# FFN up: the third pair of columns as plain products instead of seven block products

## The chip, the cores and the metric

The kernel runs on one core of one Trainium2 chip. The metric is the device time of one execution in microseconds (us). TensorE (PE in the profile) multiplies, VectorE (DVE) and ScalarE (ACT) do the elementwise work, GpSimd (POOL) very little, and SyncE (SP) issues the loads. Each engine runs its instructions in the order of its own queue, and semaphores join them.

## The reference, cut to what matters

The reference is a trunk of two layers on 512 tokens of 1024 features, all in float32. Each layer has a mixer (attention and a state space model in layer 0, a gated recurrence in layer 1) and a feed-forward block (FFN), with an RMS norm before and after each:

```python
def swiglu(x, w_gate, w_up, w_down):
    return (jax.nn.silu(x @ w_gate) * (x @ w_up)) @ w_down

        hn = rms_norm(x, norm_ffn_pre[layer])
        ff = swiglu(hn, ffn_w_gate[layer], ffn_w_up[layer], ffn_w_down[layer])
        x = x + rms_norm(ff, norm_ffn_post[layer])
```

`w_gate` and `w_up` are 1024 x 2816 each, so there are 22 blocks of 128 gate columns and 22 blocks of 128 up columns. One gate block and the up block of the same number are called a pair here, numbered from 0 to 21. The change touches the two products `x @ w_gate` and `x @ w_up`, in both layers.

## The kernel before

**Numbers in two parts.** The kernel keeps x transposed: `xT` is 8 tiles of 128 features by 512 tokens. For a product in full precision each operand is split into a rounded part (`hi`, written by ScalarE as fp32r) and the rest (`lo`, a subtraction on VectorE). `mm3` (line 275) then makes three matmuls: hi with hi, hi with lo, lo with hi. For x the parts are `xh` and `xl`, for the weights `whi` and `wlo`. A `Chunk` (line 221) is a split weight block: 1024 x 128 weights lie in two tiles of 128 x 512, so one block costs two copies on ScalarE (L240) and two subtractions on VectorE (L241). A `Raw` (line 205) is such a block as loaded, two loads of 256 KB.

**Plain pairs.** The first four blocks, pairs 0 and 1, are computed plainly: 8 steps over the features, three matmuls each, 512 tokens wide. `half_cols` (line 555) does this in two halves of 256 tokens, because the norm before it delivers x in halves; the first half runs inside `out_proj`, the second in `gemm_cols` (line 571). `gemm_cols` is a generator: it stops after the second half, and what follows (the evacuation of the four banks, and further plain blocks if its list is longer) is done when `ffn_up` runs it on, at line 678.

**Block pairs.** From pair 2 on, the two blocks of a pair are treated as one product of 2 x 2 blocks (two halves of the features, gate and up, two halves of the tokens) by the Strassen-Winograd scheme with 7 block products instead of 8. `pair_weights` (line 636) loads both blocks, makes four sums of weight blocks on VectorE (L644 to L647), and splits the seven weight blocks: `a` (gate), `c` and `b` (sums) and `d` (what is left of up). The products need sums of x too: t1, t2, t3, t4, made once per layer in the loop at line 659. ScalarE writes two scaled tiles `xa`, `xb` per step, VectorE makes four sums (L666 to L669), and the sums are split into `th`, `tl` (L673, L674). The sum `t0` becomes t1: its two parts are written over the second half of `xh[k]` and `xl[k]` for k from 0 to 3, which the plain pairs have then read.

Each of the seven products is 4 steps of three matmuls, 256 wide (line 690). They go into four PSUM banks in the order 11, t2, t1, 21, t3, 22, t4 as the program is written; ScalarE copies three partial results out (L707, L709, L711) and VectorE combines them in seven operations of 128 x 256 (L720 to L726). `gated` (line 613) applies the activation and multiplies gate by up into a `hh` tile (L616).

**Buffers.** The split weights and raw blocks live in a list of named buffers, `places`: 22 in the pool `sb` and 10 in the pool `hp` of the layer, later joined by those `hh` buffers whose hidden tile comes late. `place` takes the first one free in program order (or the first one in `sb` if asked), and a load into a buffer waits until its last reader is done. Pair 2's split weights are the exception: they have `hh` buffers of their own (the iterator `own`, line 650), and its raw blocks come from `sb`, so that they can be loaded early.

**Order.** The program is written in dependence order, and a scheduler of the framework fixes the order of each engine's queue ahead of time by priorities (program order) and modelled times. Around the norm (in `out_proj`) the order is pinned by hand; in the up phase it isn't. On the chip each queue runs in that fixed order, whatever is late.

Of the kernel before, what the change touches and what calls it, by code (L numbers as in the profile page):

```python
# [11 lines left out]
F32 = mybir.dt.float32  # L12
F32R = mybir.dt.float32r
I32 = mybir.dt.int32
AF = mybir.ActivationFunctionType
ALU = mybir.AluOpType
# [3 lines left out]
P = 128  # L20
S = 512
D = 1024
NF = D // P
NT = S // P
HID = 2816
NH = HID // P
# [68 lines left out]
def hybrid_trunk(  # L95
# [9 lines left out]
    dve, act, pool = nc.vector, nc.scalar, nc.gpsimd  # L105
    sb = ctx.enter_context(tc.tile_pool(name="sb", bufs=1))
# [14 lines left out]
    def bank(name, use="main"):  # L121
        q = sets[use]
        q.append(q.pop(0))
        return psum.tile([P, 512], F32, tag=f"bank{q[-1]}", name=name)
# [16 lines left out]
    def step_one():  # L141
        due, _, gen = heapq.heappop(steps)
        clock[0] = max(clock[0], due)
        try:
            start(gen, next(gen))
        except StopIteration:
            pass

    def tick():
        while steps and steps[0][0] <= clock[0]:  # L150
            step_one()
# [34 lines left out]
    HT = S // 2  # L186
# [12 lines left out]
    def give(ps):  # L199
        places.extend(p for p in ps if p not in retired)  # L200
# [55 lines left out]
    def wchunk(src, nk, n, nm, **kw):  # L256
        return Chunk(Raw(nk, n, nm, src), nm, **kw)

    def wcols(w, c0, nk, nm, **kw):

        return wchunk(w[:, c0:c0 + P].rearrange("(k p) n -> p k n", p=P), nk, P, nm, **kw)
# [286 lines left out]
        return dve.scalar_tensor_tensor(l, src, g, h.bitcast(F32), op0=ALU.mult, op1=ALU.subtract)  # L548

    NFIRST = 4  # L550

    def first_cols(lst, nm, eng=None):
        return [wcols(w, c0, NF, f"{nm}{i}", base=sb, eng=eng) for i, (w, c0) in enumerate(lst[:NFIRST])]

    def half_cols(h, ws, xh, xl, bs, nm):

        if bs is None:
            bs = [bank(f"{nm}b{i}") for i in range(NFIRST)]
        for k in range(NF):
            while (h, k) not in ready:  # L560
                step_one()
            for i in range(NFIRST):
                for j, w in enumerate(ws[i](k)):
                    pe.matmul(bs[i][:, HS[h]], lhsT=w, rhs=xh[k][:, HS[h]], start=(k + j == 0), stop=False)
                tick()
            for i in range(NFIRST):
                pe.matmul(bs[i][:, HS[h]], lhsT=ws[i](k)[0], rhs=xl[k][:, HS[h]], start=False, stop=(k == NF - 1))
                tick()
        return bs

    def gemm_cols(lst, first, xh, xl, nm, evac):

        ws, bs = first
        half_cols(1, ws, xh, xl, bs, nm)
        for w2 in ws:
            w2.free()
        yield
        for i in range(NFIRST):
            evac(i, bs[i])
        for i in range(NFIRST, len(lst)):  # L580
            w2 = wcols(lst[i][0], lst[i][1], NF, f"{nm}{i}")
            b = bank(f"{nm}b{i}")
            for k in range(NF):
                mm3(b, w2(k), xh[k], xl[k], k == 0, k == NF - 1)
            w2.free()
            evac(i, b)
# [11 lines left out]
    def ffn_up(layer, xh, xl, first, nsum, nm, hp):  # L598
# [4 lines left out]
        cols2 = ffn_cols(layer)  # L603
        hidden = []
        env = {}
        HK = NF // 2
# [22 lines left out]
                act.activation(env[n][1], b, AF.Copy)  # L629
                gated(*env[n], n)  # L630

        heads = gemm_cols(cols2[:NFIRST], first, xh, xl, nm, evac)
        next(heads)
        mid()

        def pair_weights(n, alloc=None, base=None):

            r0, r1 = [Raw(NF, P, f"{nm}{n}{i}", cols2[2 * n + i][0][:, n * P:(n + 1) * P].rearrange(
                "(k p) n -> p k n", p=P), base=base) for i in range(2)]
            (a11, a12), (a21, a22) = r0.parts, r1.parts  # L640
            rs = Raw(NF, P, f"s_{nm}{n}", base=base)
            rt = Raw(HK, P, f"t_{nm}{n}")
            (s1, s4), (s2,) = rs.parts, rt.parts
            dve.tensor_tensor(s1, a21, a22, op=ALU.add)  # L644
            dve.tensor_tensor(s2, s1, a11, op=ALU.subtract)  # L645
            dve.tensor_tensor(a21, a11, a21, op=ALU.subtract)
            dve.tensor_tensor(s4, a12, s2, op=ALU.subtract)  # L647
            return [Chunk(t, f"{nm}{n}{q}", alloc=alloc) for t, q in ((r0, "a"), (rs, "c"), (r1, "d"), (rt, "b"))]

        own = iter([*range(11, NH), 3, 4, 5, 6])  # L650
        for q in range(NFIRST // 2 + 3):
            retired.add((hp, f"hh{q}"))
        wa, wc, wd, wb = pair_weights(
            NFIRST // 2, lambda name: hp.tile([P, S], F32R, tag=f"hh{next(own)}", name=name), sb)


        t1 = [(xh[k][:, HS[1]], xl[k][:, HS[1]]) for k in range(HK)]
        th, tl = [], []
        for k in range(HK):
            a = hp.tile([P, S], F32, tag=f"hh{7 + k % 2}", name=f"xa_{nm}{k}")  # L660
            b = hp.tile([P, S], F32, tag=f"hh{9 + k % 2}", name=f"xb_{nm}{k}")
            act.activation(a, xT[k], AF.Copy, scale=col("g1", layer * NF + k))
            act.activation(b, xT[k + HK], AF.Copy, scale=col("g1", layer * NF + k + HK))
            raw = Raw(4, HT, f"tr_{nm}{k}")
            (t2, t3), (t4, t0) = [(t[:, 0], t[:, 1]) for t in raw.parts]
            dve.tensor_tensor(t0, a[:, HS[1]], a[:, HS[0]], op=ALU.subtract)  # L666
            dve.tensor_tensor(t3, b[:, HS[1]], a[:, HS[1]], op=ALU.subtract)
            dve.tensor_tensor(t2, b[:, HS[1]], t0, op=ALU.subtract)
            dve.tensor_tensor(t4, t2, b[:, HS[0]], op=ALU.subtract)  # L669
            h = hp.tile([P, 3, HT], F32R, tag="tq", bufs=8, name=f"th_{nm}{k}")  # L670
            l = hp.tile([P, 3, HT], F32R, tag="tq", bufs=8, name=f"tl_{nm}{k}")
            for src, hi, lo in ((raw.parts[0], h[:, 0:2], l[:, 0:2]), (t4, h[:, 2], l[:, 2]), (t0, *t1[k])):
                act.activation(hi, src, AF.Copy)  # L673
                dve.tensor_tensor(lo, src, hi.bitcast(F32), op=ALU.subtract)  # L674
            raw.free()
            th.append(h)
            tl.append(l)
        for _ in heads:
            pass
        give([(hp, f"hh{q}") for q in range(7, NH)])  # L680
        X = {
            "11": [(xh[k][:, HS[0]], xl[k][:, HS[0]]) for k in range(HK)],
# [8 lines left out]
            for k in range(HK):  # L691
                mm3(o[:, HS[0]], w2(k0 + k), x[k][0], x[k][1], k == 0 and not onto, k == HK - 1, skip_group_check=onto)

        for n in range(NFIRST // 2, NH):
            if n > NFIRST // 2:
                for q in range(n + 3):
                    retired.add((hp, f"hh{q}"))
                places[:] = [p for p in places if p not in retired]
                wa, wc, wd, wb = pair_weights(n)
            b0, b1, b2 = [bank(f"{nm}{i}b{n}") for i in range(3)]  # L700
            b3 = side(f"{nm}3b{n}")
            e = sb.tile([P, S], F32, tag="sq", bufs=2, name=f"pu_{nm}{n}")
            p5 = sb.tile([P, HT], F32, tag="sqh", bufs=2, name=f"pv_{nm}{n}")
            p1, p6 = e[:, HS[0]], e[:, HS[1]]

            product(b0, wa, 0, X["11"])
            act.activation(p1, b0[:, HS[0]], AF.Copy)  # L707
            product(b1, wb, 0, X["t2"])
            act.activation(p6, b1[:, HS[0]], AF.Copy)  # L709
            product(b2, wc, 0, X["t1"])  # L710
            act.activation(p5, b2[:, HS[0]], AF.Copy)  # L711
            product(b0, wa, HK, X["21"], onto=True)
            product(b1, wd, 0, X["t3"], onto=True)
            product(b2, wc, HK, X["22"], onto=True)
            product(b3, wd, HK, X["t4"])
            for w2 in (wa, wc, wd, wb):
                w2.free()
            gt, ut = out_tiles(n)
            rb = env["rb"]
            dve.tensor_tensor(p6, p1, p6, op=ALU.add)  # L720
            dve.tensor_tensor(gt[:, HS[0]], b0[:, HS[0]], rb[:, HS[0]], op=ALU.mult)
            dve.tensor_tensor(p1, p1, b1[:, HS[0]], op=ALU.add)
            dve.tensor_tensor(ut[:, HS[1]], p1, p5, op=ALU.add)
            dve.tensor_tensor(p6, p6, b2[:, HS[0]], op=ALU.add)
            dve.tensor_tensor(gt[:, HS[1]], p6, rb[:, HS[1]], op=ALU.mult)
            dve.tensor_tensor(ut[:, HS[0]], p1, b3[:, HS[0]], op=ALU.subtract)  # L726
            gated(gt, ut, n)

        hh, hl = [], []
        for n in range(NH):  # L730
            if n < 4:
                h, _ = place(f"hi_{nm}{n}", F32R, hp)
            elif n < 16:
                h = sb.tile([P, S], F32R, tag="xh" if n < 12 else "xl", bufs=NF, name=f"hi_{nm}{n}")
            else:
                h = hp.tile([P, 3, HT], F32R, tag="tq", bufs=8, name=f"hi_{nm}{n}")
                h = h.rearrange("p a n -> p (a n)")[:, 0:S]
            act.activation(h, hidden[n], AF.Copy)
            if n == 0:
                l = place(f"lo_{nm}{n}", F32R, hp)[0]  # L740
            else:
                l = hp.tile([P, S], F32R, tag=f"hh{n - 1}", name=f"lo_{nm}{n}")
# [885 lines left out]
    xh, xl, first, nsum = even_layer()  # L1628
    for f in range(NF):
        dump(f"x1_{f}", xT[f])  # L1630
    xh, xl, first, nsum = ffn(0, xh, xl, first, nsum)
# [4 lines left out]
    xh, xl, first, nsum = odd_layer(xh, xl, first, nsum)  # L1636
# [34 lines left out]
```

## Time and profile before

| | us |
|---|---|
| median of 3 runs (1167.83 to 1178.44) | 1168.26 |
| the profiled execution | 1169.77 |
| its span, first to last instruction | 1167.7 |
| first block product of layer 0, pair 2 | 292.5 |
| first block product of layer 1, pair 2 | 827.9 |

A group line of the profile names the source line, the engine, the operation, the output and inputs by their tile names, shapes and a count. The banks of the block products are called f00b to f03b in layer 0 and f10b to f13b in layer 1; the plain pairs use mo0b and mo1b. A weight tile such as whi_f03c is the hi part of block c of pair 3 in layer 0. A stretch line gives, for each engine, busy time and number of instructions, then the granted TensorE clock, the share of the DMA engines and GB/s. A wait line reads: who waited, for whom, total, times, longest. TensorE's busy time is modelled: a matmul of 256 columns is shown with about 0.28 us, while the next one starts about 0.12 us after it; the distance of the starts is what counts. In square brackets stands the idle time before an instruction and what ended it.

### The profile page before, as it was taken

The numbers are of one execution on the slowest core, as the hardware profiler recorded it, in microseconds if no ns is written. First come the engines' busy times: TensorE is split into PE (matmuls) and PEld (weight loads), VectorE is DVE, ScalarE is ACT, GpSimd is POOL, SyncE is SP. The second block draws the span as 40 slices with busy tenths as digits, with TensorE's granted clock in tenths as the row PEclk, the third lists the DMA queues.
The fourth block names the chain that finished last, engine by engine and source line by source line (L and its number), as shares of the span: only waits on it lengthen the run. The fifth ranks groups of instructions, "written<-read, shape, count | busy, mean of one in ns | idle before, by whom it ended". The sixth has DMA issues, their size and how long they took to land.

```text
span 1167.7 us, 20255 instructions
## 1 busy us (share of the span) xinstructions
PE 1131.7 (97%) x7550; PEld 1013.2 (87%) x7550; DVE 876.8 (75%) x1841; ACT 626.6 (54%) x1290; POOL 60.6 (5%) x100
## 2 busy tenths in 40 slices
PE   6999899999999999999999999999999999999997
PEld 6877666889999999988889887889999999988886
DVE  7989675478999899882345887956999899984224
ACT  7556576357655555652244479744855455582221
POOL 1000010003000000000004000004000000000001
PEclk9999989999999999999999999999999999999999
DMA  8534410522333332423330323430253333334221
GB/s 211 144 117 134 108 45 1 172 64 63 93 109 100 101 99 83 125 92 96 121 100 1 106 86 98 126 109 1 77 146 95 101 109 91 90 119 126 91 63 72
DMA packets 165561, 113.45 MB, mean 97 GB/s; under 512 B 26852, under 2 KB 142296, under 8 KB 165464
## 3 DMA queue, kind: packets, MB, share of 16 engines
q1 hardware_dynamic: 162168, 109.95, 32.2%
q10 hardware_dynamic: 3040, 2.17, 0.7%
q8 instruction: 59, 0.97, 0.3%
q14 instruction: 38, 0.31, 0.1%
q0 software_dynamic: 256, 0.06, 0.0%
HBM read 103.75 MB, written 4.19 MB: 92 GB/s over the span
## 4 chain that ended last, share of the span: by engine, by line
PE 82%; DVE 5%; ACT 5%; DMA 4%; issue 2%; POOL 0%; ACTq 0%; DVEq 0%; POOLq 0%; SPq 0%
PE fo L170 10%; PE op_fd L170 10%; PE op_mo L170 6%; PE f00b L170 5%; PE f02b L170 5%; PE f01b L170 4%; PE f11b L170 4%; PE f10b L170 4%; PE f12b L170 4%; PE qkv L170 4%; PE gg L170 3%; PE f03b L170 2%; PE f13b L170 2%; PE mo1b L170 2%; PE mo0b L170 2%; PE xbb L170 2%
## 5 line engine op out<-in xcount | busy, mean ns | idle before, releaser
L241 DVE TENSOR_TENSOR wlo_fo<-wraw_fo,whi_fo 128x512 fp32r<-128x512 f32 x44 | 30.3, 691 | 63.8 <-PE fo L170 58.7
L170 PE MATMUL op_fd<-hi_f,whi_fd 128*128 128x512 f32 (+1 forms) x200 | 73.7, 369 | 0.0
L170 PE MATMUL op_fd<-lo_f,whi_fd 128*128 128x512 f32 (+1 forms) x200 | 73.4, 367 | 0.0
L170 PE MATMUL op_fd<-hi_f,wlo_fd 128*128 128x512 f32 (+1 forms) x200 | 73.0, 367 | 0.0
L170 PE MATMUL fo<-wlo_fo,hi_f 128*128 128x512 f32 x176 | 69.4, 394 | 0.0
L170 PE MATMUL fo<-whi_fo,lo_f 128*128 128x512 f32 x176 | 69.1, 394 | 0.0
L170 PE MATMUL fo<-whi_fo,hi_f 128*128 128x512 f32 x176 | 68.9, 396 | 0.0
L240 ACT ACTIVATE whi_fo<-wraw_fo 128x512 fp32r<-128x512 f32 x44 | 27.6, 631 | 70.6 <-DMA wraw_fo<-in_ffn_w_down_dram 43.4
L241 DVE TENSOR_TENSOR wlo_fd<-wraw_fd,whi_fd 128x512 fp32r<-128x512 f32 x44 | 30.1, 690 | 46.4 <-ACT whi_fd L240 42.5
L240 ACT ACTIVATE whi_fd<-wraw_fd 128x512 fp32r<-128x512 f32 x44 | 27.4, 629 | 54.7 <-DMA wraw_fd<-in_ffn_w_down_dram 33.8
L170 PEld LDWEIGHTS op_fd<-lo_f,whi_fd 128*128 128x128 f32 x200 | 37.7, 189 | 6.8
L170 PEld LDWEIGHTS op_fd<-hi_f,wlo_fd 128*128 128x128 f32 x200 | 37.7, 189 | 6.7
L170 PEld LDWEIGHTS op_fd<-hi_f,whi_fd 128*128 128x128 f32 x200 | 37.7, 189 | 6.6
L170 PE MATMUL qkv<-whi_qkv,xh_m 128*128 128x512 f32 x96 | 40.5, 427 | 0.0
L170 PEld LDWEIGHTS fo<-whi_fo,lo_f 128*128 128x128 f32 x176 | 33.1, 188 | 7.8
L170 PEld LDWEIGHTS fo<-whi_fo,hi_f 128*128 128x128 f32 x176 | 33.1, 188 | 7.7
L170 PEld LDWEIGHTS fo<-wlo_fo,hi_f 128*128 128x128 f32 x176 | 33.1, 188 | 7.5
L170 PE MATMUL qkv<-wlo_qkv,xh_m 128*128 128x512 f32 x96 | 38.3, 399 | 0.0
L170 PE MATMUL qkv<-whi_qkv,xl_m 128*128 128x512 f32 x96 | 38.0, 396 | 0.0
L644 DVE TENSOR_TENSOR wraw_s_f<-wraw_f,wraw_f 128x512 f32<-128x512 f32 x40 | 27.4, 684 | 11.4 <-DMA wraw_f<-in_ffn_w_up_dram 10.7
L241 DVE TENSOR_TENSOR wlo_mo<-wraw_mo,whi_mo 128x512 fp32r<-128x512 f32 x32 | 21.4, 686 | 14.5 <-ACT whi_mo L240 14.2
L645 DVE TENSOR_TENSOR wraw_t_f<-wraw_s_f,wraw_f 128x512 f32<-128x512 f32 x40 | 27.3, 682 | 6.0 <-DMA wraw_f<-in_ffn_w_gate_dram 6.0
(1974 smaller groups left out, 4297.8 us busy)
## 6 DMA issues: line engine op xcount, KB each, us to landing
wraw_f<-in_ffn_w_gate_dram SPq DMA_DIRECT2D x88, 256.0 KB, 3.1
wraw_f<-in_ffn_w_up_dram SPq DMA_DIRECT2D x88, 256.0 KB, 3.3
wraw_fd<-in_ffn_w_down_dram SPq DMA_DIRECT2D x44, 256.0 KB, 2.8
wraw_fo<-in_ffn_w_down_dram SPq DMA_DIRECT2D x44, 256.0 KB, 2.9
wraw_qkv<-in_ev_w_in_dram SPq DMA_DIRECT2D x24, 256.0 KB, 3.5
wraw_mo<-in_ev_w_out_dram SPq DMA_DIRECT2D x16, 256.0 KB, 4.3
wraw_xb<-in_od_w_in_dram SPq DMA_DIRECT2D x16, 256.0 KB, 2.8
wraw_gg<-in_od_w_in_dram SPq DMA_DIRECT2D x16, 256.0 KB, 2.8
```

Source lines behind the costliest of these rows:

```text
L170: self.pin(nc.tensor.matmul(o, lhsT=lhsT, rhs=rhs, start=start, stop=stop, **kw))
L240: act.activation(hi, src, AF.Copy)
L241: eng.tensor_tensor(lo, src, hi.bitcast(F32), op=ALU.subtract)
L644: dve.tensor_tensor(s1, a21, a22, op=ALU.add)
L645: dve.tensor_tensor(s2, s1, a11, op=ALU.subtract)
```

## The change

Pair 2 joins the plain pairs. `gemm_cols` gets the first six blocks instead of four; the two new ones come ready made as `plain`, two `Chunk`s that are made where pair 2's block weights were made, with raw blocks from `sb` and split parts in eight `hh` buffers (before, pair 2's seven split blocks took fourteen). Pair 3 is now the first block pair; its weights are prepared after the block sums of x, before the evacuations, from the common list of buffers. Since the plain products of pair 2 read both halves of `xh` and `xl`, t0 can't be split at once any more: it is kept in two buffers of its own (`z`), and its split into t1 stands behind the plain products.

```diff
     NFIRST = 4
+    NPLAIN = 3
...
-    def gemm_cols(lst, first, xh, xl, nm, evac):
+    def gemm_cols(lst, first, xh, xl, nm, evac, ready_w=None):
...
         for i in range(NFIRST, len(lst)):
-            w2 = wcols(lst[i][0], lst[i][1], NF, f"{nm}{i}")
+            w2 = ready_w(i) if ready_w else wcols(lst[i][0], lst[i][1], NF, f"{nm}{i}")
             b = bank(f"{nm}b{i}")
...
-        heads = gemm_cols(cols2[:NFIRST], first, xh, xl, nm, evac)
+        heads = gemm_cols(cols2[:2 * NPLAIN], first, xh, xl, nm, evac, lambda i: plain[i - NFIRST])
...
-        own = iter([*range(11, NH), 3, 4, 5, 6])
-        for q in range(NFIRST // 2 + 3):
+        own = iter(range(11, NH))
+        for q in range(NPLAIN + 3):
             retired.add((hp, f"hh{q}"))
-        wa, wc, wd, wb = pair_weights(
-            NFIRST // 2, lambda name: hp.tile([P, S], F32R, tag=f"hh{next(own)}", name=name), sb)
+        plain = [Chunk(Raw(NF, P, f"{nm}p{i}", cols2[i][0][:, cols2[i][1]:cols2[i][1] + P].rearrange(
+            "(k p) n -> p k n", p=P), base=sb), f"{nm}p{i}",
+            alloc=lambda name: hp.tile([P, S], F32R, tag=f"hh{next(own)}", name=name))
+            for i in range(NFIRST, 2 * NPLAIN)]
...
+        z = Raw(HK, HT, f"tz_{nm}")
+        z0 = [z.parts[k // z.step][:, k % z.step] for k in range(HK)]
         for k in range(HK):
...
-            (t2, t3), (t4, t0) = [(t[:, 0], t[:, 1]) for t in raw.parts]
+            (t2, t3), (t4, _) = [(t[:, 0], t[:, 1]) for t in raw.parts]
+            t0 = z0[k]
...
-            for src, hi, lo in ((raw.parts[0], h[:, 0:2], l[:, 0:2]), (t4, h[:, 2], l[:, 2]), (t0, *t1[k])):
+            for src, hi, lo in ((raw.parts[0], h[:, 0:2], l[:, 0:2]), (t4, h[:, 2], l[:, 2])):
                 act.activation(hi, src, AF.Copy)
                 dve.tensor_tensor(lo, src, hi.bitcast(F32), op=ALU.subtract)
...
+        wa, wc, wd, wb = pair_weights(NPLAIN)
         for _ in heads:
             pass
+
+        for k in range(HK):
+            act.activation(t1[k][0], z0[k], AF.Copy)
+            dve.tensor_tensor(t1[k][1], z0[k], t1[k][0].bitcast(F32), op=ALU.subtract)
+        z.free()
         give([(hp, f"hh{q}") for q in range(7, NH)])
...
-        for n in range(NFIRST // 2, NH):
-            if n > NFIRST // 2:
+        for n in range(NPLAIN, NH):
+            if n > NPLAIN:
```

## The prediction

> **What bounds the kernel now.** I read the page's first part and its chain of waits, then the busy times in stretches of 10 us through both FFN up phases, then what TensorE waited for at the start of each phase, and last the queues of VectorE, ScalarE and SyncE there.
>
> ```profile
> span 1167.7 us, 20255 instructions
> PE 1131.7 (97%) x7550; PEld 1013.2 (87%) x7550; DVE 876.8 (75%) x1841; ACT 626.6 (54%) x1290; POOL 60.6 (5%) x100
> PE 82%; DVE 5%; ACT 5%; DMA 4%; issue 2%; POOL 0%; ACTq 0%; DVEq 0%; POOLq 0%; SPq 0%
> ```
>
> TensorE sets the time, so an edit pays only where it removes TensorE work or a hole in it. This edit adds TensorE work; the holes must pay for it. In the stretches below the first pair of numbers is TensorE's busy time and its count of matmuls. At 340 to 350 us the up phase runs without a hole.
>
> ```profile
> 300.00:310.00 10.00, 9.33 (x76) 8.86 (x74) 10.00 (x18) 6.91 (x13) 0.00 (x0) 1.00 0.24 69
> 310.00:320.00 10.00, 8.65 (x70) 8.46 (x71) 9.56 (x20) 4.65 (x10) 0.00 (x0) 1.00 0.49 143
> 340.00:350.00 10.00, 10.00 (x86) 10.00 (x85) 10.00 (x20) 5.91 (x14) 0.00 (x0) 1.00 0.30 86
> 470.00:480.00 10.00, 9.18 (x77) 8.97 (x76) 9.64 (x19) 4.75 (x11) 0.00 (x0) 1.00 0.36 105
> 830.00:840.00 10.00, 7.96 (x62) 7.31 (x61) 9.75 (x19) 9.97 (x21) 0.00 (x0) 1.00 0.07 19
> 850.00:860.00 10.00, 9.52 (x79) 9.32 (x79) 10.00 (x21) 5.51 (x11) 0.00 (x0) 1.00 0.62 173
> 860.00:870.00 10.00, 9.87 (x83) 9.68 (x82) 10.00 (x21) 6.09 (x13) 0.00 (x0) 1.00 0.30 83
> 980.00:990.00 10.00, 9.20 (x77) 9.00 (x77) 10.00 (x21) 5.77 (x12) 0.00 (x0) 1.00 0.24 69
> ```
>
> Against 86 matmuls per 10 us, the start of layer 0's phase lacks 10 + 16 = 26 and that of layer 1 lacks 24 + 7 + 3 = 34. I count missing matmuls rather than idle time, because after each stop the next matmuls also come further apart than in a full stream. VectorE, the third pair of numbers, is full in nearly all of these stretches. What ended the holes (first two rows layer 0, the others layer 1):
>
> ```profile
> PE f02b L170 <- ACT whi_f03c L240: 1.0, 1, 1.0
> PE f01b L170 <- ACT pu_f L709: 1.0, 1, 1.0
> PE f11b L170 <- DVE tl_f L674: 1.1, 1, 1.1
> PE f13b L170 <- DVE ut_f L726: 0.5, 1, 0.5
> PE f10b L170 <- ACT pu_f L707: 0.5, 1, 0.5
> PE f10b L170 <- DVE wlo_f13a L241: 0.4, 1, 0.4
> ```
>
> These are weight splits, block sums of x and evacuations: work of VectorE and ScalarE that is late at the start of the phase.
>
> **The change part by part.** *TensorE.* Per layer, 7 products of 4 k-steps of 3 matmuls, 84 of 256 columns, give way to 2 columns of 8 k-steps of 3, 48 of 512 columns. Both prices stand in the chain:
>
> ```profile
> 353.06 1.43 PE f01b L170 x12
> 655.13 22.15 PE xbb L170 x96
> ```
>
> A 256-wide one takes 1.43/12 = 0.119 us and a 512-wide one 22.15/96 = 0.231 us. So 48 x 0.231 = 11.07 us stand against 84 x 0.119 = 10.01 us: +1.06 us per layer, +2.1 us for both, all of it on the path. The Trainium skill, page "TensorE: Matmul & The Clock Gate", section "Back-to-back issue gap", gives columns/2.4 + 2.5 ns, thus 215.8 and 109.2 ns; by it the edit would add 1.19 us per layer and the sum below would be 0.3 us worse. The trace's 231 and 119 ns lie above both figures, so the rows stand.
>
> *The holes.* 26 + 34 = 60 missing matmuls x 0.119 = 7.1 us (3.1 and 4.0). Whether they close is a matter of VectorE's ledger. Prices, from the chain, are 0.60 us for a 512-wide operation (1.20 for two) and 0.34 for a 256-wide one:
>
> ```profile
> 835.29 1.20 DVE gt_f L627 x2
> 850.88 0.34 DVE pu_f L720
> 279.77 0.68 DVE L645 TENSOR_TENSOR wraw_t_f<-wraw_s_f,wraw_f 128x512 f32<-128x512 f32 x1
> 284.38 0.41 DVE L666 TENSOR_TENSOR wraw_tr_f<-xa_f 128x256 f32<-128x256 f32 x1
> 304.89 0.42 DVE L674 TENSOR_TENSOR tl_f<-wraw_tr_f,th_f 128x256 fp32r<-128x256 f32 x1
> 292.75 1.45 PE f00b L170 x12
> ```
>
> In layer 0 the block sums start at 284.38 and end at 304.89. From 284.38 until TensorE can begin pair 4, VectorE now owes: block sums 4 x (6 x 0.34 + 0.60) = 10.6; the last two splits of pair 2, 1.2; four sums and seven splits each for pairs 3 and 4, 13.2; evacuation of the first two pairs, 2.4; that of pair 2, 7 x 0.34 + 0.60 = 3.0. In all 30.4 us, done at 314.8. TensorE without holes would reach pair 4 at 292.7 + 2 x 10.0 = 312.7, so VectorE is about 2 us late, which fits the 3.1 us lost. After the change pair 2 costs 4 splits instead of 4 sums and 7 splits before that point, and 1.2 of evacuation. Of those 11 operations 7 lay in VectorE's queue from 279.77 up to the first block sum, 4.2 us, where now 4 lie, 2.4 us; so the block sums can begin 1.8 us sooner, at 282.6. Then it owes: block sums without t0's split 4 x (5 x 0.34 + 0.60) = 9.2; pairs 3 and 4, 13.2; three plain evacuations, 3.6; the four moved splits, 1.4. In all 27.4, done at 310.0, while TensorE reaches pair 4 at 292.7 + 11.1 + 10.0 = 313.8. Two us late become almost 4 us early, and pair 3 too has 11 us of plain matmuls as cover. ScalarE loses 7 + 3 copies per layer and gains 4 + 1; it was not full in layer 0 after 300 us. I take the holes as closed, but keep one stop of 0.4 us per layer, the smallest of the waits above, for the new seam between plain and block products: 7.1 - 0.8 = 6.3 us back. Bounds: nothing back, to all 7.1.
>
> *The moved split.* Four ScalarE copies and four VectorE subtractions of 256 columns per layer now wait for the plain products, since they overwrite the second half of xh and xl.
>
> ```profile
> 832.08 0.41 ACT L673 ACTIVATE xh_mo<-wraw_tr_f 128x256 fp32r<-128x256 f32 x1
> 833.07 0.42 DVE L674 TENSOR_TENSOR xl_mo<-wraw_tr_f,xh_mo 128x256 fp32r<-128x256 f32 x1
> ```
>
> They touch k 0 to 3 only, so the last matmul that they wait for is 4 k-steps, 12 x 0.231 = 2.8 us, before the end of the plain ones. One copy and four subtractions take 0.41 + 4 x 0.42 = 2.1 us, and the products 11 and t2 stand ahead of t1, 2 x 1.43 us more. Queued behind them are the evacuation of the third pair and the splits of pair 4, both with slack by the ledger. I take 0; if this cover went, the price is a late tl_f as in the row of 1.1 us above, per layer.
>
> *Loads and buffers.* The third pair still loads four blocks of 256 KB through SyncE; POOL gets nothing. Two buffers more are held for t0 until the moved splits. Pair 3's gate blocks take the two sb buffers left free, but its up blocks must, as I read the order of the list, wait for buffers of the first columns.
>
> ```profile
> 287.60 4.30 SPq L216 DMA_DIRECT2D wraw_f<-in_ffn_w_up_dram  x3
> wraw_f<-in_ffn_w_up_dram SPq DMA_DIRECT2D x88, 256.0 KB, 3.3
> 826.94 3.19 DMA wraw_f<-in_ffn_w_up_dram
> 830.25 0.69 DVE L644 TENSOR_TENSOR wraw_s_f<-wraw_f,wraw_f 128x512 f32<-128x512 f32 x1 [1.06 <-DMA wraw_f<-in_ffn_w_up_dram]
> 831.19 1.02 DVE L674 TENSOR_TENSOR tl_f<-wraw_tr_f,th_f 128x512 fp32r<-128x512 f32 x2
> ```
>
> In layer 1 such a load held VectorE for 1.06 us at 829, and tl_f, behind it in the queue, is what TensorE then waited for. After the change the load may be as late, but pair 3 is wanted 11 us later: 0, bounded by the same wait.
>
> **Sum.** +2.1 - 6.3 = -4.2 us. The profiled execution took 1169.77 us (its span of 1167.7 and 2.1 around it), so 1165.6 on its scale; the median of the runs shown is 1168.26, 1.5 us lower, and I predict for it: 1168.26 - 4.2 = 1164.1 us.
>
> **The rivals.** *The queue's order holds TensorE, not the amount of work.* Then a late load or copy in a strict queue stops it as before, and the longer matmuls come on top. For it speaks the wait of 1.06 us above, and that ScalarE was far from full at 310 to 320 (4.65 of 10). Against it: VectorE had under half a microsecond free per 10 us there. Nothing comes back: +2.1, 1170.4 us, slower than before. It decides once less than 2.1 of the 7.1 us returns. The same page of the Trainium skill ("Architectural detail") has VectorE and ScalarE as strict first-in first-out; the trace agrees, tl_f at 831.19 running only behind the blocked sum.
>
> *The stop moves to the seam.* Pair 3's up blocks come late and hold VectorE in front of the block sums, or t1 is late: one stop per layer like the one of 1.1 us, with 0.3 for the restart. That is 1.4 instead of 0.4 twice: -2.2, 1166.0 us. For it: SyncE's three issues at 287.60 took 4.30 us, waiting for buffers. Against it: the 11 us of cover.
>
> *The lead lasts.* VectorE's lead also closes the late holes at 470 to 480 and 980 to 990, 9 matmuls each, 18 x 0.119 = 2.1 us, and no seam is left: 2.1 - 7.1 - 2.1 = -7.1, 1161.1 us. Against it: 100 us of full VectorE lie between, in which pairs cost it 11 x 0.60 + 7 x 0.34 + 0.60 = 9.6 of TensorE's 10.0 us, so a lead would grow, but those waits may come from buffers.
>
> **How the numbers follow.** Forecast 0.50, seam 0.22, order of the queues 0.15, lasting lead 0.13. The range runs from the lasting lead, 1161.0, to 1168.5, halfway between the seam and the queue rival, and leaves out 0.15. Faster or slower by over 1%, which is about what a measurement of this kernel can tell from no change, means 11.7 us. No case comes near it: the holes hold 9.2 us together, the added work is 2.1. I leave 0.01 for faster and 0.02 for slower, for an order of instructions that turns out otherwise in a whole phase.
>
> **What would show it.** Right: 48 matmuls of 128x512 in about 11.1 us ahead of f03 and f13; no TensorE wait above 0.5 us in the 30 us behind them; block sums done some 10 us sooner than 304.89; VectorE no longer full in those stretches. Wrong: waits of about 1 us on f0 or f1 banks behind whi, tl or pu; a first t1 product held by xl; TensorE's busy time up by 2 us with the same counts of missing matmuls.

## The result and the profile after

The kernel before took 1171.28 us and the changed one 1165.95 us (medians of 18 runs each); the ratio is 0.9944, 95% interval 0.9922 to 0.9966, that is 6.6 us less with 4 to 9 as its bounds; the medians differ by 5.3 us. The prediction was 1164.1 us, 4.2 less than a start of 1168.26, the median of 3 runs; the 18 runs put that start 3.0 us higher. Two later comparisons beside the kernel before gave 0.993 and 0.9935. One run of e2, an experiment below, took 3862.53 us and one of b4 2822.71; both are left out of all figures.

The first part and the summary of the chain, from the page of the changed kernel:

```profile
span 1165.9 us, 20079 instructions
PE 1135.2 (97%) x7478; PEld 1014.8 (87%) x7478; DVE 865.5 (74%) x1815; ACT 623.5 (53%) x1280; POOL 60.2 (5%) x100
PE 86%; ACT 5%; DMA 4%; DVE 3%; issue 1%; ACTq 0%; POOL 0%; DVEq 0%; POOLq 0%; SPq 0%
```

TensorE's busy time rose by 3.5 us with 72 matmuls fewer, VectorE's fell by 11.3, and VectorE's share of the chain went from 5% to 3%. The plain pair in the chain of waits of the changed kernel, layer 1 as the example (start, length, matmuls):

```profile
829.42 11.20 PE f1b L170 x48
```

The same kernel in stretches (TensorE's busy time and its matmuls come first):

```profile
300.00:310.00 10.00, 10.00 (x71) 9.27 (x70) 10.00 (x20) 9.25 (x19) 0.00 (x0) 1.00 0.12 35
310.00:320.00 10.00, 10.00 (x86) 10.00 (x85) 10.00 (x20) 5.32 (x11) 0.00 (x0) 1.00 0.46 133
470.00:480.00 10.00, 7.74 (x51) 7.33 (x50) 7.14 (x14) 3.77 (x8) 0.00 (x0) 0.83 0.29 83
...
1010.00:1020.00 10.00, 8.62 (x71) 8.22 (x71) 8.78 (x17) 6.03 (x13) 0.00 (x0) 1.00 0.34 108
```

The starts of both up phases are full: 71 matmuls from 300 to 310 because some are still 512 wide, then 86. The late holes are still there, and in this execution that of layer 0 is larger than before (51 matmuls for 77). What TensorE waited for from 440 to 520 us, and the one wait that counts in layer 1:

```profile
PE f00b L170 <- ACT whi_f021a L240: 2.0, 1, 2.0
PE f01b L170 <- ACT pu_f L721: 0.7, 2, 0.5
...
PE f12b L170 <- ACT whi_f120c L240: 1.3, 1, 1.3
```

**Where the time went, by phase.** A phase is read from the broadcast of the norm (bc_f, eight matmuls in each layer) to the last matmul of the down product. The row of bc_f gives the first of the eight in layer 0 and the last of the eight in layer 1, which starts 0.8 us behind that layer's first in each of these kernels. The rows of the kernel before, then of the changed one (smallest, median and largest duration in ns, first and last start in us):

```profile
L170 PE MATMUL bc_f<-cst,rsy_f x16: 272/275/275, 291.7 to 827.9; 128*128 128x128 f32 x16
...
L170 PE MATMUL op_fd<-hi_f,wlo_fd x200: 277/392/422, 494.8 to 622.8; 128*128 128x512 f32 x76, 128*128 128x256 f32 x24
...
L170 PE MATMUL fo<-whi_fo,lo_f x176: 387/394/400, 1034.9 to 1160.5; 128*128 128x512 f32 x176
```

```profile
L170 PE MATMUL bc_f<-cst,rsy_f x16: 272/275/275, 291.5 to 829.1; 128*128 128x128 f32 x16
...
L170 PE MATMUL op_fd<-hi_f,wlo_fd x200: 279/392/401, 493.2 to 624.5; 128*128 128x512 f32 x76, 128*128 128x256 f32 x24
...
L170 PE MATMUL fo<-whi_fo,lo_f x176: 387/393/402, 1031.3 to 1158.7; 128*128 128x512 f32 x176
```

Layer 0 took 622.8 - 291.7 = 331.1 us before and 333.0 after, layer 1 332.6 and 329.6. Read in the same way, with c0 as a second profile of the kernel before and a0 and c1 as two more of the changed one (the experiments below):

| us | before, c0 | after, a0, c1 | change predicted |
|---|---|---|---|
| layer 0, up and down | 331.1, 331.0 | 333.0, 329.1, 332.9 | 1.06 - 3.1 + 0.4 = -1.6 |
| layer 1, up and down | 332.6, 332.7 | 329.6, 329.0, 329.2 | 1.06 - 4.0 + 0.4 = -2.5 |

Layer 1 gained 3.0 to 3.7 us, a little more than predicted. Layer 0 gained 2.0 once and lost 1.9 twice. By these two lines the median should have moved by 1 to 6 us. A part of the rest lies ahead of layer 0's phase.

**A gain that the prediction did not have.** VectorE's timeline of the kernel before, at the end of the mixer of layer 0, 40 us ahead of the up phase (in brackets the idle time ahead of an instruction and what ended it):

```profile
250.33 0.69 DVE L644 TENSOR_TENSOR wraw_s_f<-wraw_f,wraw_f 128x512 f32<-128x512 f32 x1 [2.25 <-DMA wraw_f<-in_ffn_w_up_dram]
250.94 0.42 DVE L532 TENSOR_TENSOR oacc_mo<-oacc_mo,oqs_mo 128x256 f32<-128x256 f32 x1
```

L644 is the first weight sum of the third pair. It stands in VectorE's queue among the mixer's last sums and waits 2.25 us for a load; oacc_mo behind it is late, and TensorE waits for it (waits of the kernel before, 240 to 262 us):

```profile
PE cs_mo L170 <- DVE oacc_mo L532: 0.9, 1, 0.9
PE cs_mo L170 <- ACT oqs_mo L530: 0.5, 1, 0.5
```

TensorE's busy time from 244 to 292 us, first before, then in a0, a run of the changed kernel; both had the full clock there:

```profile
244.00:292.00 48.00, 45.62 (x382) 44.96 (x381) 35.89 (x85) 29.30 (x68) 14.41 (x17) 1.00 0.21 61
```

```profile
244.00:292.00 48.00, 47.01 (x393) 46.42 (x392) 35.90 (x86) 31.27 (x70) 14.41 (x17) 1.00 0.21 62
```

A plain pair has no such sum, so 1.4 us of idle time go. All four profiles here that have the third pair in blocks (before, c0, e1, e2) have the wait on oacc_mo, 0.8 to 2.0 us; none with it plain has it. In layer 1 the same L644 stands at 780.68 and cost TensorE only 0.3 us.

### The profile page after: what moved, and what is told of

The parts are those of the page before. It is cut to its first block, busy times and chain, and to the rows that moved or that the text cites. A ratio compares the mean times of both kernels' runs of the same rounds, so it can differ in the third digit from the quotient of the medians.

```text
span 1165.9 us, 20079 instructions
## 1 busy us (share of the span) xinstructions
PE 1135.2 (97%) x7478; PEld 1014.8 (87%) x7478; DVE 865.5 (74%) x1815; ACT 623.5 (53%) x1280; POOL 60.2 (5%) x100
## 4 chain that ended last, share of the span: by engine, by line
PE 86%; ACT 5%; DMA 4%; DVE 3%; issue 1%; ACTq 0%; POOL 0%; DVEq 0%; POOLq 0%; SPq 0%
PE fo L170 10%; PE op_fd L170 10%; PE op_mo L170 7%; PE f10b L170 5%; PE f00b L170 4%; PE f11b L170 4%; PE f01b L170 4%; PE f12b L170 4%; PE f02b L170 4%; PE qkv L170 4%; PE gg L170 3%; PE f13b L170 2%; PE f03b L170 2%; PE mo0b L170 2%; PE fd0b L170 2%; PE xbb L170 2%
## 5 line engine op out<-in xcount | busy, mean ns | idle before, releaser
L617 DVE TENSOR_TENSOR hh_f<-ut_f,gt_f 128x512 f32<-128x512 f32 x44 | 30.2, 685 | 1.6 <-ACT gt_f L615 1.5
```

Of the source, the lines that this page charges most:

```text
L617: dve.tensor_tensor(h, ut, gt, op=ALU.mult)
```

## The experiments

All ratios are to the kernel before, measured beside the run, and are ratios of mean times. The last column is read from the profiled execution as above.

| run | edit | us, median | ratio, 95% interval | layers 0 + 1, us |
|---|---|---|---|---|
| before | | | 1 | 331.1 + 332.6 |
| a0 | the changed kernel | 1161.99 | 0.993 [0.9905, 0.9955] | 329.1 + 329.0 |
| e1 | before, pair 10 plain instead of the third | 1167.76 | 0.9984 [0.9961, 1.0006] | 331.5 + 332.3 |
| e2 | before, block sums on GpSimd | 1179.94 | 1.0082 [1.005, 1.0114] | 337.6 + 339.3 |
| e3 | changed, 12 more VectorE operations per layer | 1172.73 | 1.0034 [1.0008, 1.006] | 333.7 + 331.4 |
| b1 | changed, one more buffer | 1157.37 | 0.9853 [0.9822, 0.9885] | 329.3 + 326.9 |
| b2 | changed, hidden buffers kept longer | 1158.94 | 0.9877 [0.9853, 0.9901] | 330.2 + 328.2 |
| b3 | changed, fourth pair plain too | 1159.34 | 0.9879 [0.9847, 0.9911] | 328.4 + 328.1 |
| b4 | changed, pair 10 plain too | 1157.01 | 0.9871 [0.9835, 0.9908] | 328.8 + 328.6 |
| c0 | before again | 1168.00 | 0.9978 [0.9948, 1.0008] | 331.0 + 332.7 |
| c1 | changed again | 1163.93 | 0.9935 [0.9907, 0.9964] | 332.9 + 329.2 |
| c2 | b1 again | 1160.20 | 0.9885 [0.9843, 0.9927] | 328.9 + 326.8 |
| c3 | b3 again | 1154.40 | 0.9855 [0.9818, 0.9892] | 328.4 + 328.0 |

### The changed kernel again

> The changed kernel once more, beside the kernel before. Ledger theory (VectorE owes the start of each up phase about 6 us less): ratio 0.994 to 0.997, the first 30 us behind the plain pair free of TensorE waits above 0.5 us in both layers again, and a late hole again before pair 21's first product, because its load waits for a buffer that pair 19 frees. Rival (the late hole was an accident of one execution): the waits behind whi_f021a and whi_f120c fall under 0.5 us in this trace.

The starts were full again, and the ratio agrees. The late hole of layer 0 was not the same; it is taken up below.

### Was it VectorE's work or the order of the queues?

*e1* leaves the third pair in blocks and computes pair 10 plainly (there the second half of x is partly the block sum, so two columns have other values):

```diff
                 places[:] = [p for p in places if p not in retired]
+                if n == 10:
+                    for i in (2 * n, 2 * n + 1):
+                        w2 = wcols(cols2[i][0], cols2[i][1], NF, f"{nm}p{i}")
+                        o = bank(f"{nm}b{i}")
+                        for k in range(NF):
+                            mm3(o, w2(k), xh[k], xl[k], k == 0, k == NF - 1)
+                        w2.free()
+                        evac(i, o)
+                    continue
```

> The kernel before with pair 10 computed plainly instead of pair 2 (its second token half meets t1 in place of x for half of the features, so the outputs differ; the work is the same in size). The same TensorE work is added and the same VectorE work removed, but 80 us behind the start. Ledger theory: the holes at the start stay (26 and 34 missing matmuls), the plain pair costs its 1.2 us per layer, so +2 to +3 us against before, ratio 1.001 to 1.004. Rival (VectorE is relieved anywhere, the place does not matter): as the change, ratio 0.994 to 0.997.

The ratio came out between the two. Stretches of e1:

```profile
300.00:310.00 10.00, 8.10 (x66) 7.62 (x65) 9.81 (x19) 5.04 (x11) 0.00 (x0) 1.00 0.58 164
470.00:480.00 10.00, 10.00 (x87) 10.00 (x86) 10.00 (x21) 7.08 (x14) 0.00 (x0) 1.00 0.35 98
```

The start's hole stayed, as the ledger said, but this doesn't speak for the ledger alone: TensorE's order at the start is that of the kernel before, with waits on the same two tiles (whi_f03c 0.9 us, pu_f 1.0), and any cause that lies there would have stayed. The phase also began 4.6 us sooner, so the two stretches aren't quite the same work. The late hole went, which neither theory had. The added 2.4 us and the late holes about cancel. So place matters: here a plain pair closed a hole behind it, not those ahead.

*e2* takes the block sums off VectorE in another way, with TensorE's work as before:

```diff
-            dve.tensor_tensor(t0, a[:, HS[1]], a[:, HS[0]], op=ALU.subtract)
+            pool.tensor_tensor(t0, a[:, HS[1]], a[:, HS[0]], op=ALU.subtract)
...
-            dve.tensor_tensor(t4, t2, b[:, HS[0]], op=ALU.subtract)
+            pool.tensor_tensor(t4, t2, b[:, HS[0]], op=ALU.subtract)
```

> The kernel before with the four block sums of x per step on GpSimd instead of VectorE: 16 operations of 0.34 us per layer leave VectorE's queue, 5.4 us, and nothing is added on TensorE. Ledger theory: at least two thirds of the 7.1 us at the starts come back, -4 to -6 us, ratio 0.995 to 0.9965. Rival (order of the queues or late loads hold TensorE): within 1 us of before, ratio 0.999 to 1.001. Second rival (GpSimd at 0.9 us per sum is itself late): TensorE waits behind tl_f and th_f grow beyond 1.1 us and the ratio lies above 1.

The groups of GpSimd in e2 and its stretch from 290 us (each of the four sums has four instructions; the numbers are the total in us and the mean in ns):

```profile
L666 POOL TENSOR_TENSOR wraw_tr_f<-xa_f 128x256 f32<-128x256 f32 x4 | 4.3, 1084 | 4.5 <-issue 4.5
...
L669 POOL TENSOR_TENSOR wraw_tr_f<-wraw_tr_f,xb_f 128x256 f32<-128x256 f32 x4 | 3.3, 834 | 0.2
```

```profile
290.00:300.00 10.00, 6.69 (x47) 6.28 (x46) 8.70 (x10) 8.84 (x20) 9.33 (x10) 0.85 0.19 54
```

VectorE was no longer full (8.70), but GpSimd now nearly was (9.33), at two to three times VectorE's 0.34 to 0.41 us per sum, and VectorE's subtractions behind it were later: the last tl_f of layer 0 starts at 308.79 instead of 304.89. The second rival's ratio came true, but not its wait: 0.9 us on tl_f, where the large ones in layer 0 were on weight splits (wlo_f03a 2.4, whi_f05b 1.8). The run shows nothing for or against the ledger: it put a slower engine in the same place.

*e3* was meant as the direct test. It makes the four low-part subtractions of each layer's two plain blocks four times over, 12 more operations of 0.60 us, 7.2 us per layer (the word "eight" in its expectation should read "four"):

```diff
-            alloc=lambda name: hp.tile([P, S], F32R, tag=f"hh{next(own)}", name=name))
+            alloc=lambda name: hp.tile([P, S], F32R, tag=f"hh{next(own)}", name=name), again=3)
...
-                    eng.tensor_tensor(lo, src, hi.bitcast(F32), op=ALU.subtract)
+                    for _ in range(1 + again):
+                        eng.tensor_tensor(lo, src, hi.bitcast(F32), op=ALU.subtract)
```

> The changed kernel with each of the eight low-part subtractions of the two plain blocks of pair 2... made four times per tile (12 more operations of 0.60 us per layer, 7.2 us, in front of the block sums). Nothing else moves. Ledger theory: the lead of 3.8 us turns into a lateness of about 3.4 us, so the holes at the start come back with 2 to 4 us per layer: +4 to +8 us against the changed kernel, ratio to before 0.998 to 1.003. Rival (the gain came from buffers and loads, not from VectorE): as the changed kernel within 1.5 us, ratio 0.993 to 0.997.

```profile
310.00:320.00 10.00, 8.83 (x67) 8.26 (x68) 10.00 (x20) 6.67 (x15) 0.00 (x0) 1.00 0.25 72
```

That stretch of e3 has 67 matmuls where the changed kernel has 86, though e3's phase begins 5 us later (bc_f at 296.7 for 291.5). Holes came back: idle time at the start is 2.2 us in layer 0 and 3.4 in layer 1. The ledger had a lead of 3.8 us; 7.2 more make it 3.4 late, which fits. But e3 took 10.7 us more than a0, where 4 to 8 were expected, and its ratio lies above the expected range too.

Nor is it a clean test. Although the edit adds operations on VectorE alone, the scheduler then fixed other orders for VectorE, ScalarE and TensorE: 10 of the plain matmuls of layer 0 and 11 of layer 1 run ahead of the broadcast, 2.3 and 2.6 us that the table's phases of e3 leave out. And of its waits in layer 0, the one of 1.0 us on whi_f04c came from ScalarE after ScalarE itself had waited 1.74 us for TensorE, and one on pu_f came behind a gate load for which ScalarE had waited 1.95 us. More work on VectorE and another order came together, and the run doesn't tell them apart.

### The late holes

The changed kernel's timelines of SyncE, ScalarE and TensorE at 469 us, cut to the chain of pair 21's first weights:

```profile
469.32 0.37 SPq L216 DMA_DIRECT2D wraw_f<-in_ffn_w_gate_dram  x1
...
474.85 1.15 ACT L240 ACTIVATE whi_f021a<-wraw_f 128x512 fp32r<-128x512 f32 x2 [5.54 <-DMA wraw_f<-in_ffn_w_gate_dram]
...
475.53 0.39 PE L170 MATMUL f00b<-xh_mo,whi_f021a 128*128 128x256 f32 x1 [1.98 <-ACT whi_f021a L240]
```

The load lands 5.5 us after its issue, and ScalarE and TensorE stand still for it. In a0 the same load was issued as far into the phase (468.51 - 290.7 = 177.8 us; here 469.32 - 291.5 = 177.8):

```profile
468.51 0.37 SPq L216 DMA_DIRECT2D wraw_f<-in_ffn_w_gate_dram  x1
...
472.01 1.15 ACT L240 ACTIVATE whi_f021a<-wraw_f 128x512 fp32r<-128x512 f32 x2 [3.51 <-DMA wraw_f<-in_ffn_w_gate_dram]
```

There it took 3.5 us, and the wait on whi_f021a was gone. c1 (5.56) went as the first profile. So whether this kernel has the hole in layer 0 goes by the landing time of one load that is issued with no room. Why that takes 3.5 us in one execution and 5.5 in another, the traces don't show. There is no room because of the order too: two matmuls of pair 21's first product stand in TensorE's queue 182.0 us into the phase (a0; 184.0 in the changed kernel, behind the wait), and the ten others only from 188.6 us on (192.1). Four edits bear on it.

```diff
-EXTRA = 10
+EXTRA = 11
```

> The changed kernel with EXTRA at 11 instead of 10: one more 128x512 buffer in the pool from which raw blocks and weight splits are taken. Theory: the late hole (pair 21 in layer 0, pair 20 or 21 in layer 1) is a gate load that SyncE can issue only when the weights of two pairs before free a buffer, so one buffer more lets it go out sooner: the waits on whi_f021a and whi_f120c of 1 to 2 us go or halve, and the time falls by 1 to 3 us against the changed kernel; with its ratio of 0.993 to 0.994 that makes 0.990 to 0.993. Rival: VectorE and ScalarE are late there by work, not by loads; then the waits and the time stay, 0.993 to 0.995.

```diff
-                for q in range(n + 3):
+                for q in range(n + 1):
                     retired.add((hp, f"hh{q}"))
```

> The changed kernel with the buffers of the hidden columns taken out of the weight pool two pairs later (n + 1 instead of n + 3 at pair n). Theory of the late buffers: two more buffers in each of the last pairs, so the late holes close: 460 to 500 and 980 to 1020 us at 85 or 86 matmuls per 10 us, clock 1.00 there, the time 1 to 4 us below the changed kernel, ratio 0.989 to 0.993. Rival (work, not loads): unchanged, 0.993 to 0.995. Third way: the evacuation of a pair now waits for the weights that still lie in its hidden buffer; new waits in VectorE, ratio 0.995 or more.

```diff
-    NPLAIN = 3
+    NPLAIN = 4
...
-        heads = gemm_cols(cols2[:2 * NPLAIN], first, xh, xl, nm, evac, lambda i: plain[i - NFIRST])
+        heads = gemm_cols(cols2[:2 * NPLAIN], first, xh, xl, nm, evac, lambda i: plain[i - NFIRST] if i < NFIRST + 2 else
+                          wcols(cols2[i][0], cols2[i][1], NF, f"{nm}p{i}"))
...
-            for i in range(NFIRST, 2 * NPLAIN)]
+            for i in range(NFIRST, NFIRST + 2)]
```

> The changed kernel with the fourth pair plain as well. Ledger: the holes at the starts are closed already, so a second plain pair can only cost: 48 x 0.233 instead of 84 x 0.119 per layer, +1.2 each, +2.4 us in all against the changed kernel, ratio 0.995 to 0.997, start stretches full as they are now. Rival (the lead of VectorE lasts and reaches the late holes, since it falls behind by nothing in between): the late stretches fill too and 2 to 4 us come back there, ratio 0.991 to 0.994.

b4 is the changed kernel with the lines of e1:

> The changed kernel with pair 10 computed by plain products too (the second half of x is partly the block sum there, so the two columns' values are not the reference's; the amount of work is). Ledger by stretch: +2.4 us for the two layers. In the run with pair 10 plain and pair 2 in blocks the late holes were gone; if a lead gained at pair 10 closes them, 2 to 4 us come back and the sum lies between -1.6 and +0.4 against the changed kernel, ratio 0.991 to 0.995, with 85 or 86 matmuls per 10 us from 460 to 510 and from 970 to 1040. Rival (they were gone by chance of the order of loads): the late holes stay and the ratio is 0.995 to 0.997.

All four came out at 0.985 to 0.988, better than any number expected. Since the changed kernel had not been run beside them, two were repeated with it:

> The kernel before once more, for a second profile of it. Idle time of TensorE in the 200 us of each up phase was 2.8 and 3.7 us in the first profile (4.5 of the 6.5 at the starts) and 2.7 + 1.4 and 0.9 + 1.1 in the two profiles of the changed kernel, all of it late in the phases. Theory (the holes at the starts belong to the kernel's order, those late in the phases vary from execution to execution): starts again at 4 to 5 us idle, late ones anywhere from 0 to 4 us. Rival (the starts vary as well, and the first profile was an extreme): less than 3 us idle at the starts. Ratio 0.998 to 1.002 either way.

> The changed kernel, third time, beside the same runs of the kernel before: ratio 0.992 to 0.995 and starts without idle time. It is the measure for the two kernels with it here. If the chip or the hour made the four kernels of the last call look good, it comes out at 0.988 or less as well.

> EXTRA at 11 again, now beside the changed kernel. Its up phases had 0.9 us of idle time in all against 2.0 and 4.1 in the changed kernel. Theory of the late buffers: 1 to 4 us below the changed kernel, the late holes gone again. Rival (its 0.985 was the hour): within 1 us of the changed kernel, and late holes of a microsecond back.

> The fourth pair plain too, again, beside the changed kernel. Its up phases had no idle time at all. +2.4 us of TensorE work; the late idle time of 2.0 to 4.1 us with the slower restart behind it gives back 2.5 to 5. Theory (VectorE's lead lasts and closes the late holes): 0 to 3 us below the changed kernel. Rival (only the extra work counts, the last call was the hour): 1 to 3 us above it.

c0 repeats the holes of the kernel before almost to the matmul (c0's stretches; 76, 70 and 77 matmuls in the first profile):

```profile
300.00:310.00 10.00, 9.41 (x76) 8.95 (x75) 10.00 (x18) 7.01 (x14) 0.00 (x0) 1.00 0.23 67
310.00:320.00 10.00, 8.69 (x70) 8.48 (x71) 10.00 (x22) 4.71 (x10) 0.00 (x0) 1.00 0.51 145
470.00:480.00 10.00, 9.18 (x77) 8.96 (x76) 9.65 (x19) 4.77 (x11) 0.00 (x0) 1.00 0.36 105
```

So the count on which the prediction stood was no accident of one execution. c1 came out at 0.9935, so there is no sign that the hour made the other four look good. The late stretch of c2, with one more buffer:

```profile
470.00:480.00 10.00, 10.00 (x86) 10.00 (x85) 7.51 (x15) 4.37 (x11) 0.00 (x0) 1.00 0.37 107
```

In b1 and c2 no late hole is left in either layer, and the two phases take 655.7 to 656.2 us against 658.1 to 662.6. c2 took 3.7 us less than c1, within the 1 to 4 expected, though their intervals overlap. But the way was not the expected one: the load of pair 21 goes out no sooner (180.3 us into the phase in b1 and 179.9 in c2, for 177.8). It is the two matmuls that stand 5 us later (187.6 and 187.2 us into the phase). One buffer more changed the order of the queues, and with that order the hole closed. In b2 the wait on whi_f021a is gone too, but waits of 1.0 to 1.5 us on pv_f stand at 348 and 491 us and in layer 1: its third way in kind, though the two phases still took only 658.4 us. c3's chain and its late stretch:

```profile
291.48 11.20 PE f0b L170 x48
303.03 11.18 PE f0b L170 x48
```

```profile
470.00:480.00 10.00, 10.00 (x87) 10.00 (x86) 10.00 (x21) 5.78 (x12) 0.00 (x0) 1.00 0.40 114
```

Two plain pairs per layer leave no idle time in either up phase, though they cost 2.4 us more, and the two phases are as short as with one buffer more. A lead of VectorE that lasts would do that. But the order differs here too: in b3, c3 and b4 no part of pair 21's first product runs early any more; it starts 192.9 to 193.2 us into the phase, more than 10 us behind the issue of its load. Lead and order were not told apart. The numbers expected of both edits were too cautious.

**The best of them.** c3 took 1154.40 us where the changed kernel took 1163.93 and the kernel before 1170.51; its interval, 0.9818 to 0.9892, lies wholly below the changed kernel's, 0.9907 to 0.9964. That is 9.5 us less, where 0 to 3 were expected. Its phases explain 329.2 + 332.9 - 656.4 = 5.7 us of them. The rest may be the clock: the median run was granted 0.9945 in c3 and 0.9895 in c1. Whether fewer holes keep the clock up or the hour did is open. Fourth pair plain and a further buffer together were not tried.

## Why the prediction was right

The number was right. The reason given for it is borne out in layer 1; in layer 0 other rows held TensorE, and two terms that the prediction had not seen offset each other.

- *The plain pair*, +1.06 us per layer: 11.20 us for 48 matmuls against 11.07 worked out, so +1.2 per layer and +2.4 in all. The step held, 0.3 us short.
- *The holes at the starts*, 6.3 of 7.1 us back: all of it came back. No wait on TensorE is left from 288 to 340 or from 826 to 880 us, so the 0.4 us per layer kept for the new seam was not needed.
- *VectorE's ledger*, from 2 us late to 4 early. In layer 1 of the kernel before, the chain of waits goes through VectorE's operations almost without a break from 830.25 to 857.5 us, behind a load that landed at 830.1; there the ledger is borne out, for 34 of the 60 missing matmuls, though 1.06 us of VectorE's lateness was its wait for that load. In layer 0 it is not. From 292.75 to 318 us that chain has no piece of VectorE: TensorE is followed at 307.82 by 3.64 us of a gate load, then by ScalarE. VectorE's and ScalarE's rows there, in the kernel before:

```profile
307.04 0.68 DVE L647 TENSOR_TENSOR wraw_s_f<-wraw_f,wraw_t_f 128x512 f32<-128x512 f32 x1
...
309.16 0.63 ACT L240 ACTIVATE whi_f05a<-wraw_f 128x512 fp32r<-128x512 f32 x1 [1.29 <-DMA wraw_f<-in_ffn_w_gate_dram]
309.70 0.61 ACT L240 ACTIVATE whi_f03c<-wraw_s_f 128x512 fp32r<-128x512 f32 x1
311.55 0.63 ACT L240 ACTIVATE whi_f06a<-wraw_f 128x512 fp32r<-128x512 f32 x1 [1.24 <-DMA wraw_f<-in_ffn_w_gate_dram]
312.08 0.61 ACT L240 ACTIVATE whi_f05a<-wraw_f 128x512 fp32r<-128x512 f32 x1
312.60 0.37 ACT L709 ACTIVATE pu_f<-f01b 128x256 f32<-128x256 f32 x1
```

  The two tiles that TensorE waited for, whi_f03c and pu_f, stand in ScalarE's queue behind splits of pairs 5 and 6, and these waited for gate loads. VectorE's sum for whi_f03c was done at 307.7, before ScalarE came to it; c0 and e1 show the same two waits on loads, 1.2 us each. In the changed kernel the load of pair 5 goes out at 295.19 instead of 305.93 us, and ScalarE waits for it while TensorE has work:

```profile
298.21 0.63 ACT L240 ACTIVATE whi_f05a<-wraw_f 128x512 fp32r<-128x512 f32 x1 [2.93 <-DMA wraw_f<-in_ffn_w_gate_dram]
```

  So the sum "2 us late, which fits the 3.1 us lost" fits layer 0 by luck. The lead of 4 us isn't seen there either: VectorE's last split for pair 4 ended at 311.3 us before, ahead of TensorE's start on that pair at 314.5, and at 314.9 after, behind a start at 311.9. The block sums end at 296.8 + 0.4 instead of 304.9 + 0.4, 8 us sooner and not 10, but they begin only 1.1 us sooner (283.30 for 284.38), so most of the 8 is another order of the queue and not less work. Which of order and buffers made the gate loads early was not tested by itself. One sign was wrong: VectorE is still full (10.00) from 300 to 320.
- *The moved split and the loads*, 0: right at the starts; no wait behind xl or t1 is seen.
- *What was left out, a gain*: the prediction counted VectorE's seven operations of the third pair ahead of the block sums only as work, from 279.77 us on. Another, L644 at 250.33, lies outside its count, and held the mixer's sums behind it for a load. That is 1.4 us of idle time, and about 2 us by six executions with the full clock there: from the last three splits of the first columns to bc_f it took 47.2, 47.0 and 47.0 us with the third pair in blocks (before, e1, e2) and 45.0, 44.9 and 45.2 with it plain (a0, b3, b4). The Trainium skill, page "TensorE: Matmul & The Clock Gate", section "Architectural detail", has VectorE as strict first-in first-out; the row at 250.33 agrees. The prediction quoted that rule for a rival against the change and did not look where it worked for it. The cause rests on the wait being there in the four profiles with the third pair in blocks and gone in all others; moving L644 alone was not tried.
- *What was left out, a loss*: the late holes were taken as unchanged (or, in a rival, as closed). Idle time from 100 to 200 us into the phase went from 0.8 us to 2.7 in layer 0 in two of three executions, with a lower clock behind it.
- *The sum*: +2.4 - 7.1 at the starts, -2 ahead of layer 0, and 0 to +4 late in layer 0 give -7 to -3; 5 to 8 us less were measured. The -4.2 came near it because the two missing terms have opposite signs, one of -2 and one of up to +4; it is luck in part. The level of 1164.1 us also rests on a start that was 3.0 us too low; from 1171.28 the same -4.2 gives 1167.1. The upper end of the range, too, is not the halfway point that it is said to be: between 1166.0 and 1170.4 that is 1168.2, not 1168.5.
- *The rivals*: the price of the rival on the queues' order fell, since the holes closed, but its mechanism is what the rows of layer 0 show: a late load in a strict queue, with TensorE's tiles behind it. It missed that the edit would also change the order and the buffers. The stop at the seam fell. The lasting lead fell for this kernel, which still has late holes; with two plain pairs the stretches came out as it says, but whether by the lead or by the order is open.

## What to carry to other kernels

An operation that waits for a load, placed early in a strict queue, costs whoever stands behind it; when it goes, look for the gain there, even 40 us ahead of the code that was changed. Before booking a hole to the engine with the most work, follow the chain to the row that held the awaited tile: layer 0's holes looked like VectorE's and stood behind loads in ScalarE's queue. Added TensorE work paid here where it stood in front of holes, not behind them; that part of this is a new order of the queues must be looked for in the profile, since one edit can rewrite all of them. Before counting a hole as a fixed cost, see in a second profile whether it repeats (those at the starts did, almost to the matmul) or comes and goes with one load's landing (2 us either way).

## What was not expected of the hardware

The granted clock fell to half behind the late hole, in the changed kernel's stretches of 1 us:

```profile
475.00:476.00 1.00, 0.47 (x2) 0.30 (x2) 0.49 (x1) 1.00 (x3) 0.00 (x0) 1.00 0.75 218
476.00:477.00 1.00, 0.71 (x4) 0.68 (x4) 1.00 (x3) 1.00 (x4) 0.00 (x0) 0.67 0.00 0
...
479.00:480.00 1.00, 1.00 (x8) 1.00 (x7) 1.00 (x2) 0.00 (x0) 0.00 (x0) 0.62 0.00 0
480.00:481.00 1.00, 1.00 (x11) 1.00 (x10) 1.00 (x4) 0.00 (x0) 0.00 (x0) 1.00 0.00 0
```

From 476.3 to 479.8, 3.4 us, 6 to 8 matmuls stand in a microsecond where 11 had, and half of it, 1.7 us, is lost on top of the hole of 2.3 (10 - 7.74, from the stretch of 470 to 480). The three executions with idle time of over 2 us there (after, c1, e3) have it; a0, with 0.3 and 0.7 in two stretches, does not. The Trainium skill, page "TensorE: Matmul & The Clock Gate", section "What's actually happening", has the clock halve after an idle window of about 3.4 us; the length of the halved stretch agrees, but here 2.3 us of idle time were enough. Nor is 2 us a fixed bound: TensorE of the kernel before stood idle for 2.04 us from 830 to 840 and kept the clock at 1.00, and e2 fell to half for 3.4 us after 1.87 us of idle time from 320 to 330. The clock also fell where no such hole was (0.66 from 260 to 265 us in the changed kernel), so holes are not its only cause.

One load of 256 KB, issued at the same point of the same kernel, took 3.5 us in one execution and 5.5 in two others. GpSimd needs 0.83 to 1.08 us for a 128x256 sum that VectorE does in 0.41 by its rows.
